# Two hybrid decoder layers on one core: whole-array products with zero rows and columns, one exponent matrix per delta head, and the sample attention's packed products in one run

## The chip, the core and the metric

The kernel runs on one core of a Trainium2 chip. The metric is the device time of one execution in microseconds (us), median of several runs. The core has five engines with a queue each: TensorE (PE; its weight loads are listed apart as PEld), VectorE (DVE), ScalarE (ACT), GpSimd (POOL) and SyncE (SP), which in this kernel issues nearly all DMAs.

## What is computed

Two layers of a decoder, for a prompt of 512 tokens and for 8 samples of 8 tokens (64 tokens); model width 1024, all float32. A layer does this:

```
h = rmsnorm(x);  one input projection, cut into the inputs of three branches and three gates
A: 4 heads HGRN2, gated linear recurrence, per-channel decay
B: 4 heads differential attention (two halves of 64 per head), QK norm, rotary;
   a sample also attends to 1024 past positions in paged caches
C: 4 heads gated DeltaNet: conv, l2 norm of q and k, per-head decay g, and per block of 128 tokens
   D = exp(G_t - G_s);  A = beta D (k k^T), strictly lower;  U = (1 + A)^-1 beta (v - e^G k S)
   o = e^G q S + ((q k^T) D) U
x = x + (sum of sigmoid(gate) * (branch @ w_branch)) @ w_out
x = x + (silu(conv(g)) * u) @ w_down        with g, u = rmsnorm(x) @ w_up
```

Outputs are the new x, the final states of the branches, the new key and value rows and the convolution histories.

## The kernel before, in words

All 576 tokens (512 and 64) stand in the free dimension, 128 channels on the partitions. **Dense products** (`dense_steps`, L265) make one output tile of 128 channels: the float32 weights are loaded by SP (`raw`), split into a high and a low float32r part by ACT (`wh`) and DVE (`wl`), and for each of the K blocks six matmuls of 288 columns run on the whole 128x128 array (two halves of the tokens, three products of high and low parts). Such a matmul is called a dense pass below. One tile of `w_out`, the first of layer 0, is cut in 512 and 64 columns instead (`wide`).

**The branch stage** of a layer mixes the 68 tiles of the input projection with everything that the branches need. `drive` (L319) is a planner that runs while the program is written: it has three lanes of Python generators (left and right: the heads; `smp`: the samples one after another, as soon as the attention heads have ended) and a clock that counts estimated PE time. A head says `yield 4.2` when its next step should come 4.2 us of that clock later, or asks for a dense tile with `yield win(i)`; in between, the planner emits dense passes, one K block at a time, gates and output gates (`fill`) when no head asks. What the program is handed to afterwards is a tile scheduler that may still change the order of instructions on an engine.

The **small products** of the heads are plain float32. Each shows in the trace as two passes (a float32 transpose is one). They use the array in several shapes, which the trace gives as rows*columns: 128*128 (whole), fewer rows where a product sums over 64 tokens (or over 15 bf16 rows), fewer columns where the left operand has 64 of them, and 128*32 or 64*128 or 32*128 where several products are packed side by side (`tile_position`). PSUM for them is `rp()`, four banks in turn.

What the change touches:

- `transpose_to` (L470) and `transpose_back` (L485): four transposes of 128 tokens, and one for the 64 sample tokens.
- `gdn_head` (L752): `parts` (L784) cuts an exponent vector into three bf16 parts, `weights` (L795) transposes them (`pst`), spreads them over the partitions by five products with 15 rows (`sel`, `rt`), multiplies k by k (call 0) or k by q (call 1) and applies exp. Call 0 is followed by the triangular solve of 16x16 blocks: `da` goes to DRAM and back, 30 DVE instructions on `dtr` (L855), `dt` and `ct` to DRAM and back, then `TB`, whose first use on PE is L913. Call 1 comes after the solve in the code, behind `yield 1.0` and `yield 4.5`; `yield 1.0` and `yield 11.0` come before `TB` is used.
- `gdn_head`'s end (L974 to L984): two products of 64x64 for the samples. `hgrn_head` (L990): `level` (L1026) has a sample product with 64 columns at three of its seven levels, and `ATs` (L1119) one of 64x64.
- `diff_head`: `scores` (L1204), two packed products of 64 rows for each of four query blocks, then softmax.
- `diff_sample` (L1256), for each sample: K pages loaded, `sn` (new keys, packed 128*32), `yield 7.0`, `sc` for the first four pages, `yield 7.0`, V pages 0, `sc` for the other four, softmax, V pages 1, transposes, `po` (packed; its last step has 64 rows), `ob`, `yield 1.2`, a packed product with `comb`. The four products `sn`, `sc`, `sc`, `comb` are apart from each other.

Of the kernel before, what the change touches and what calls it, by code (L numbers as in the profile page):

```python
# [10 lines left out]
F32 = mybir.dt.float32  # L11
# [17 lines left out]
HALF = T // 2  # L29
PAST = 1024  # L30
# [115 lines left out]
def kernel(ctx, tc, a, o, depth=DEPTH, dbg=None):  # L146
# [118 lines left out]
    def dense_steps(src, xs, M=128, raws=None, nk=None, prime=False, wide=False):  # L265
# [23 lines left out]
        for g, (k0, n) in enumerate(gr):  # L289
            wh, wl = nxt  # L290
            for i in range(n):
# [4 lines left out]
                for w, xx in ((wh, (xh, xl)), (wl, (xh,))):  # L296
                    for hf in range(2):
                        for x_ in xx:
                            ts = (slice(0, SEQ), slice(SEQ, T))[hf] if wide else slice(hf * HALF, (hf + 1) * HALF)
                            mm(acc[:M, hf, :ts.stop - ts.start], w[:, cs], x_[:, ts],  # L300
                               start=(k == 0 and w is wh and x_ is xh), stop=(k == nk - 1 and w is wl))
# [3 lines left out]
        if wide:  # L305
            return acc.rearrange('p a b -> p (a b)')[:, 0:T].rearrange('p (a b) -> p a b', a=2)
        return acc[:, :, :HALF]

    def dense(src, xs, wide=False):
        return run(dense_steps(src, xs, wide=wide))  # L310
# [119 lines left out]
    def norm_sq(k, xt, sqp, sa):  # L430
        if k == 0:
            S.activation(sa, xt, AF.Square)
        else:
            sq = sqp.tile([128, T], F32, tag='sq', bufs=2, name='sq')
            S.activation(sq, xt, AF.Square)
            tt(sa, sa, sq, ALU.add)
# [4 lines left out]
    def norm_stats(sa, rb, r):  # L441

        ps = rp()
        for j in range(5):
            n = 128 if j < 4 else NS
            mm(ps[:n, j:j + 1], sa[:, 128 * j:128 * j + n], ones[:, 0:1])
# [23 lines left out]
    def transpose_to(dst, src, scale=None):  # L470
# [4 lines left out]
        trp(ps2[:NS, 0:128], src[:, SEQ:], ident)  # L475
        G.memset(dst[NS:, 4, :], 0.0)
        if scale is None:
            S.copy(dst[:, 0:4, :], ps.rearrange('p (j d) -> p j d', j=4))
            S.copy(dst[:NS, 4, :], ps2[:NS, 0:128])
# [3 lines left out]
        S.activation(dst[:NS, 4, :], ps2[:NS, 0:128], AF.Copy, scale=scale[:NS, 4:5])  # L483

    def transpose_back(src):  # L485
# [4 lines left out]
        trp(ps2[:, 0:NS], src[:NS, 4, :], ident[:NS, :NS])  # L490
        return ps, ps2[:, 0:NS]

    def head_norm(ot, p):
# [10 lines left out]
    def finish_gated(ot, key, src, gcol, dst, p, tag):  # L504
# [3 lines left out]
        head_norm(ot, p)  # L508
# [81 lines left out]
    with stage('ln0', 'right') as p0:  # L590
        sa = p0.tile([128, T], F32, tag='sqa', name='sqa')
# [45 lines left out]
    for l in range(depth):  # L637
# [10 lines left out]
        bh = lay.tile([128, 5, 4], F32, tag='bh', name='bh')  # L648
# [4 lines left out]
        GB = lay.tile([128, 5, 4], F32, tag='GB', name='GB')  # L653
        GC = lay.tile([128, 5, 4], F32, tag='GC', name='GC')
# [19 lines left out]
        def decays(p):  # L674
# [9 lines left out]
            S.activation(bh, sp[:, :, 0:4], AF.Exp, scale=-1.0)  # L684
            V.tensor_scalar(out=bh, in0=bh, scalar1=0.5, scalar2=None, op0=ALU.mult)
# [3 lines left out]
            lab = lay.tile([NS, NB, 4], F32, tag='lab', name='lab')  # L689
            tt(lab, bc1(la[:NS, 4, :], NB), bc(c['bm8'][:NS], 4), ALU.mult)  # L690
# [4 lines left out]
            mm(ps[:, 32:64], ones[:NS, :], lab.rearrange('p b e -> p (b e)'))  # L695
            mm(ps[:NS, 64:68], c['trib'][:NS], la[:NS, 4, :])
            mm(ps[:NS, 68:72], c['oneb'][:NS], la[:NS, 4, :])
# [6 lines left out]
            tt(GB, Gt, sp[:, :, 0:4], ALU.subtract)  # L704
            V.tensor_scalar(out=GC, in0=Gt, scalar1=-0.5 * math.log(128.0), scalar2=None, op0=ALU.add)
            V.tensor_scalar(out=nG, in0=Gt, scalar1=-1.0, scalar2=None, op0=ALU.mult)
# [45 lines left out]
        def gdn_head(h, p):  # L752
            ckq = p.tile([128, 2, T], F32, tag='ckq', name='ckq')
            cv = p.tile([128, T], F32, tag='hn', name='cv')
            sel = c['sel'].rearrange('p (j t) -> p j t', j=5)
            mad = c['madd'].rearrange('p (a t) -> p a t', a=2)
# [858 lines left out]
```

## Time and profile before

| | us |
|---|---|
| median of 3 runs (2520.1 to 2521.52) | 2520.16 |
| the profiled execution, its own time | 2517.85 |
| its span from first to last instruction | 2516.1 |
| PE busy / DVE busy / ACT busy / POOL busy | 2492.3 / 1677.5 / 1134.2 / 119.3 |
| branch stage of layer 0 and of layer 1 (from the span's start) | 5.8 to 717 and 1266 to 1966 |

The granted TensorE clock is 0.999 of full speed. In a row of the timeline the first number is the start from the span's beginning, the second how long the row lasts, and xN the number of instructions in it. Matmul ends are modelled and overlap the next ones, so PE's cost of something is read from starts: from a start ahead of it to a start behind it, less what else was started in between.

### The profile page before, as it was taken

The numbers are of one execution on the slowest core, as the hardware profiler recorded it, in microseconds if no ns is written. First come the engines' busy times: TensorE is split into PE (matmuls) and PEld (weight loads), VectorE is DVE, ScalarE is ACT, GpSimd is POOL, SyncE is SP. The second block draws the span as 40 slices with busy tenths as digits, with TensorE's granted clock in tenths as the row PEclk, the third lists the DMA queues.
The fourth block names the chain that finished last, engine by engine and source line by source line (L and its number), as shares of the span: only waits on it lengthen the run. The fifth ranks groups of instructions, "written<-read, shape, count | busy, mean of one in ns | idle before, by whom it ended". The sixth has DMA issues, their size and how long they took to land.

```text
span 2516.1 us, 52047 instructions
## 1 busy us (share of the span) xinstructions
PE 2492.3 (99%) x19714; PEld 2338.6 (93%) x19714; DVE 1677.5 (67%) x4218; ACT 1134.2 (45%) x2435; POOL 119.3 (5%) x378
## 2 busy tenths in 40 slices
PE   8999999999999999999999999999999999999999
PEld 7898888888899999999998988888889999999999
DVE  7777777777765663646676877777686656636463
ACT  5556555556433332323455565646464333323232
POOL 1000000000000010101000000000000000101010
PEclk9999999999999999999999999999999999999999
DMA  6233464545365324242432235554534653242423
GB/s 206 88 109 120 141 202 133 181 156 177 104 213 173 133 85 159 85 146 95 137 130 95 96 121 181 168 176 148 180 129 160 192 176 119 86 159 82 159 85 124
DMA packets 222843, 352.93 MB, mean 140 GB/s; under 512 B 36864, under 2 KB 71680, under 8 KB 222592
## 3 DMA queue, kind: packets, MB, share of 16 engines
q1 hardware_dynamic: 221008, 346.78, 42.3%
q8 instruction: 156, 2.56, 0.4%
q10 hardware_dynamic: 1584, 2.82, 0.4%
q14 instruction: 95, 0.78, 0.1%
HBM read 288.90 MB, written 60.60 MB: 139 GB/s over the span
## 4 chain that ended last, share of the span: by engine, by line
PE 93%; DVE 4%; ACT 2%; issue 1%; DMA 0%; SPq 0%; ACTq 0%; DVEq 0%
PE acc L188 75%; PE r L188 14%; PE r L192 4%; DVE mx L1216 1%; DVE wl L195 0%; ACT P L1219 0%; DVE r L195 0%; DMA x<-in_xT 0%; DVE mx L1289 0%; DMA pg<-in_v 0%; ACT ks L777 0%; DVE ca L743 0%; DVE thb L723 0%; DVE xl L427 0%; DVE ro L195 0%
## 5 line engine op out<-in xcount | busy, mean ns | idle before, releaser
L188 PE MATMUL acc<-xh,wh 128*128 128x288 f32 x3584 | 1026.1, 301 | 2.9 <-DVE thb L710 1.6
L188 PE MATMUL acc<-xl,wh 128*128 128x288 f32 x3584 | 1010.7, 297 | 1.0 <-DVE xl L427 0.9
L188 PE MATMUL acc<-xh,wl 128*128 128x288 f32 x3584 | 773.3, 296 | 5.3 <-DVE wl L195 5.3
L262 ACT CAST wh<-raw 128x512 fp32r<-128x512 f32 x624 | 383.5, 615 | 841.0 <-PE acc L188 791.8
L188 PEld LDWEIGHTS acc<-xh,wh 128*128 128x128 f32 x3584 | 674.5, 188 | 33.8 <-issue 19.4
L188 PEld LDWEIGHTS acc<-xl,wh 128*128 128x128 f32 x3584 | 675.5, 188 | 6.4 <-issue 2.9
L188 PEld LDWEIGHTS acc<-xh,wl 128*128 128x128 f32 x3584 | 576.7, 188 | 11.9 <-DVE wl L195 6.5
L195 DVE TENSOR_TENSOR wl<-raw,wh 128x512 fp32r<-128x512 f32 x624 | 423.2, 679 | 187.7 <-ACT wh L262 183.7
L188 PE MATMUL acc<-hl,wh 128*128 128x288 f32 x704 | 197.5, 296 | 0.0
L188 PE MATMUL acc<-hh,wh 128*128 128x288 f32 x704 | 196.7, 294 | 0.0
L188 PE MATMUL acc<-hh,wl 128*128 128x288 f32 x704 | 150.7, 295 | 0.0
L188 PEld LDWEIGHTS acc<-hh,wh 128*128 128x128 f32 x704 | 132.2, 188 | 0.0
L188 PEld LDWEIGHTS acc<-hl,wh 128*128 128x128 f32 x704 | 132.0, 188 | 0.0
L188 PEld LDWEIGHTS acc<-hh,wl 128*128 128x128 f32 x704 | 113.9, 189 | 0.0
L188 PE MATMUL acc<-oL,wh 128*128 128x288 f32 x384 | 108.0, 295 | 0.0
L188 PE MATMUL acc<-oh,wh 128*128 128x288 f32 x384 | 107.3, 295 | 0.0
L195 DVE TENSOR_TENSOR cbf<-acc,rb 128x288 f32<-128x288 f32 x132 | 39.1, 352 | 90.2 <-PE acc L188 86.3
L1456 DVE SCALAR_TENSOR_TENSOR caf<-cbf,fm,caf 128x592 f32<-128x592 f32 x88 | 73.5, 835 | 15.1 <-ACT caf L1454 13.5
L188 PE MATMUL acc<-oh,wl 128*128 128x288 f32 x384 | 81.6, 293 | 0.0
L1412 DVE SCALAR_TENSOR_TENSOR xn<-acc,xo 128x576 f32<-128x576 f32 x40 | 30.3, 758 | 73.3 <-PE acc L188 73.3
L188 PEld LDWEIGHTS acc<-oL,wh 128*128 128x128 f32 x384 | 73.0, 190 | 0.0
L188 PE MATMUL acc<-mh,wh 128*128 128x288 f32 (+2 forms) x256 | 72.3, 296 | 0.0
(415 smaller groups left out, 3665.5 us busy)
## 6 DMA issues: line engine op xcount, KB each, us to landing
raw<-in_w_in_t SPq DMA_DIRECT2D x272, 256.0 KB
raw<-in_w_up SPq DMA_DIRECT2D x176, 256.0 KB
pg<-in_kT SPq DMA_DIRECT2D x128, 256.0 KB
pg<-in_v SPq DMA_DIRECT2D x128, 256.0 KB
raw<-in_w_dn SPq DMA_DIRECT2D x64, 256.0 KB
xo<-xres SPq DMA_DIRECT2D x56, 288.0 KB
thd<-thb SPq DMA_DIRECT2D x48, 288.0 KB
th<-thd SPq DMA_DIRECT2D x48, 288.0 KB
```

What stands on the lines that cost most here:

```text
L188: PE.matmul(out, lhsT, rhs, start=start, stop=stop, **kw)
L192: PE.transpose(out, in_, idm)
L195: (eng or V).tensor_tensor(out=out, in0=in0, in1=in1, op=op)
L262: S.copy(hi, src)
L1216: V.tensor_reduce(out=mx[:, cc:cc + 1], in_=pss[cc][:, :nk], axis=AX.X, op=ALU.max)
L1412: V.scalar_tensor_tensor(out=v2(xn), in0=acc, scalar=0.5, in1=v2(xo), op0=ALU.mult, op1=ALU.add)
L1456: V.scalar_tensor_tensor(out=A[:, 0:592], in0=P[:, j:j + 592], scalar=w[:, 3 * fi + j:3 * fi + j + 1], in1=A[:, 0:592], op0=ALU.mult, op1= ...
```

## The change

1. `wide` goes; the first tile of `w_out` is made like the others.
2. Operands of the sample products get zero rows or columns up to 128 (`TP = SEQ + 128` columns, memsets on POOL), and the products run on the whole array: the sample's transposes, `level`'s sample products, `Rs`/`TS`, `Us`/`aps`, `Vs`, the norm sums, `gsum`, part of `decays`. `ATs` is packed in 32 columns like the products that it is added to.
3. `gdn_head` makes one exponent matrix. `weights` is called once, `sel` has 128 rows, its five products stand in a run, and k is multiplied by k and q together (256 columns). What differs between the two old matrices is a factor per token, which `head_norm` takes up as `cn`. `yield 4.5` and the second call are gone.
4. `scores` makes query blocks 0 and 1 together.
5. `diff_sample` issues `comb` of the sample before, `sn` and both `sc` in one run, 12.0 after the K pages; V pages 0 are issued behind both `sc`.

```
 transpose_to:
-        trp(ps2[:NS, 0:128], src[:, SEQ:], ident)
-        G.memset(dst[NS:, 4, :], 0.0)
+        trp(ps2[:, 0:128], src[:, SEQ:], ident)
 transpose_back:
-        trp(ps2[:, 0:NS], src[:NS, 4, :], ident[:NS, :NS])
+        trp(ps2[:, 0:128], src[:, 4, :], ident)
 head_norm:
+        for _ in range(0 if cn is None else 2):
+            tt(ms, ms, cn, ALU.mult)
...
+        if cn is not None:
+            tt(r, r, cn, ALU.mult)
 gdn_head:
+            G.memset(ckq[:, :, T:], 0.0)
+            G.memset(cv[:, T:], 0.0)
...
-                trp(pst[:15, 0:128], pc.rearrange('p a j -> p (a j)'), identb)
+                trp(pst[:, 0:128], pc, identb)
...
-                pb, pg = rp(), rp()
+                pb, pg = rp(), (rp(), rp())
+                for j in range(4):
+                    mm(pb[:, 128 * j:128 * j + 128], sel[:, j, :], rt)
                 for j in range(4):
                     cs = slice(128 * j, 128 * j + 128)
-                    mm(pb[:, cs], sel[:15, j, :], rt)
-                    mm(pg[:, cs], ckq[:, 0, cs], ckq[:, i, cs])
+                    mm(pg[j // 2][:, 256 * (j % 2):256 * (j % 2) + 256].rearrange('p (i t) -> p i t', i=2), ckq[:, 0, cs], ckq[:, :, cs])
...
-            pc = parts(1)
+            cn = sm.tile([128, 5], F32, tag='cn', name='cn')
+            tt(cn, ss[:, 0], ss[:, 1], ALU.subtract)
...
-            yield 4.5
-            yield from weights(1, pc)
...
-            mm(pu[:NS, 0:128], TTs, Rs)
+            mm(pu[:, 0:128], TTs, Rs)
...
-            mm(pu[:NS, 0:128], aps[:, 1], Us)
+            mm(pu[:, 0:128], aps[:, NS:], Us)
 hgrn_head:
-                    mm(ps[:NS, :NS], lhs[:, SEQ:], rhs[:, SEQ:])
+                    mm(ps[:, :NS], lhs[:, SEQ:], rhs[:, SEQ:T])
...
-            mm(pu[:NS, 0:128], ATs, vt[:NS, 4], stop=False)
+            for q in range(2):
+                mm(pu[32 * q:32 * q + 32, 0:128], ATs[:, 32 * q:32 * q + 32], vt[:, 4], stop=False, tile_position=(0, 32 * q))
 diff_head:
-            nxt = scores(0)
+            nxt = scores(0, 1)
             for qb in range(4):
-                yield 4.2
-                P, rl = nxt
+                if qb != 1:
+                    yield 5.4 if qb == 0 else 4.2
+                P, rl = nxt.pop(0)
 diff_sample:
             Kp = [pages('K', g) for g in range(2)]
...
+            yield 12.0
             sn = rp()
+            put = combine(b - 1, sn) if b else None
             for h in range(H):
...
-            for g in range(2):
-                yield 7.0
-                if g:
-                    Vp.append(pages('V', 0))
+            scs = []
+            for g in range(2):
                 sc = rp()
                 for h in range(H):
                     mm(sc[32 * h:32 * h + 32].rearrange('p (k t) -> p k t', k=4), Qs[:, b, h, :], Kp[g][:, :, 128 * h:128 * h + 128],
                        cost=0.24, tile_position=(0, 32 * h))
+                scs.append(sc)
+            if b:
+                put()
...
+            Vp = [pages('V', 0)]
...
-                        mm(po[hs], PT[:NS, i, hs], Vs[:, h], start=False, stop=True, tile_position=(0, 32 * h))
+                        mm(po[hs], PT[:, i, hs], Vs[:, h], start=False, stop=True, tile_position=(0, 32 * h))
...
+            mm(pn[q_, 0:128], c['comb'], obs.pop(b), tile_position=(0, 32 * (b % 4)))
+            return lambda: S.copy(on[q_, b // 4], pn[q_, 0:128])
```

## Rows read from the trace of the kernel before

**Rows 1.** The page: busy time, and a group of dense passes with PE's idle before it.

```profile
PE 2492.3 (99%) x19714; PEld 2338.6 (93%) x19714; DVE 1677.5 (67%) x4218; ACT 1134.2 (45%) x2435; POOL 119.3 (5%) x378
...
L188 PE MATMUL acc<-xh,wl 128*128 128x288 f32 x3584 | 773.3, 296 | 5.3 <-DVE wl L195 5.3
```

**Rows 2.** Busy time by stretch, the two branch stages; columns as named: us, engines, clock.

```profile
5.80:717.00 711.20, 699.27 (x5710) 624.02 (x5709) 532.43 (x1610) 393.16 (x948) 32.41 (x98) 1.00 0.46 151
...
1266.00:1966.00 700.00, 693.26 (x5710) 620.02 (x5709) 520.05 (x1573) 384.31 (x932) 24.68 (x88) 1.00 0.45 146
```

**Rows 3.** PE timeline: first and second tile of `w_out`, layer 0, then layer 1.

```profile
793.25 0.39 PE L188 MATMUL acc<-mh,wh 128*128 128x512 f32 x1
...
801.41 0.38 PE L188 MATMUL acc<-mh,wh 128*128 128x288 f32 x1
...
2042.00 0.30 PE L188 MATMUL acc<-mh,wh 128*128 128x288 f32 x1
...
2048.34 0.29 PE L188 MATMUL acc<-mh,wh 128*128 128x288 f32 x1
```

**Rows 4.** PE timeline: a small product on the whole array between dense passes.

```profile
442.30 0.38 PE L188 MATMUL r<-S,ckq 128*128 128x128 f32 x2
...
442.79 0.29 PE L188 MATMUL acc<-xh,wh 128*128 128x288 f32 x1
```

**Rows 5.** PE timeline: a small product on 64*64 between dense passes.

```profile
327.29 0.29 PE L188 MATMUL acc<-xh,wh 128*128 128x288 f32 x1
327.50 0.43 PE L188 MATMUL r<-Us,aps 64*64 64x128 f32 x2
...
328.10 0.29 PE L188 MATMUL acc<-xh,wh 128*128 128x288 f32 x1
```

**Rows 6.** PE timeline: one `sc` of a sample, packed 128*32, between dense passes.

```profile
229.90 0.43 PE L188 MATMUL acc<-xh,wl 128*128 128x288 f32 x2
230.26 1.07 PE L188 MATMUL r<-pg,Qs 128*32 128x512 f32 x8
...
231.49 0.29 PE L188 MATMUL acc<-xl,wh 128*128 128x288 f32 x1
```

**Rows 7.** PE timeline: `weights`, call 0, between two times four transposes.

```profile
253.35 0.60 PE L192 MATMUL r<-cf,P 128*128 128x128 f32 x4
253.88 0.23 PE L188 MATMUL r<-rt,cb_c 15*128 15x128 bf16 x1
...
257.01 0.38 PE L188 MATMUL acc<-xh,wh 128*128 128x288 f32 x1
```

**Rows 8.** PE timeline: `weights` where the four `rt` came in a run.

```profile
386.61 0.39 PE L188 MATMUL r<-rt,cb_c 15*128 15x128 bf16 x4
...
388.43 0.53 PE L188 MATMUL acc<-xh,wl 128*128 128x288 f32 x2
```

**Rows 9.** PE timeline: five transposes, the fifth on 64 rows (64*128).

```profile
68.30 0.80 PE L192 MATMUL r<-cf,ro 128*128 128x128 f32 x5
...
69.27 0.30 PE L188 MATMUL acc<-xl,wh 128*128 128x288 f32 x1
```

**Rows 10.** PE timeline: five transposes, the fifth to 64 columns (128*64).

```profile
48.30 0.71 PE L192 MATMUL r<-cf,xr 128*128 128x128 f32 x5
...
48.98 0.30 PE L188 MATMUL acc<-xl,wh 128*128 128x288 f32 x1
```

**Rows 11.** SP's waits: us in total, times, longest; V and K pages waiting for PE.

```profile
SPq L1264 <- PE r L188: 104.4, 41, 10.3
```

**Rows 12.** DVE timeline: part of the solve, and call 1's `dd` of the same head.

```profile
386.16 1.03 DVE L195 TENSOR_TENSOR dtr<-dtr 36x15 f32<-36x15 f32 x5
387.12 0.34 DVE L809 SCALAR_TENSOR_TENSOR dd<-r,w,cb_c 128x128 f32<-128x128 f32 x1
```

**Rows 13.** DVE and PE timeline: `TB` made, and its first use.

```profile
289.58 0.89 DVE L195 TENSOR_TENSOR TB<-ctt,cf 128x128 f32<-128x128 f32 x4
...
289.94 0.63 PE L188 MATMUL r<-TB,ap 128*128 128x64 f32 x4
```

More of the change, by code (lines that the diff above doesn't have):

```diff
@@ L304, in dense_steps, with dense @@
                     yield
-        if wide:
-            return acc.rearrange('p a b -> p (a b)')[:, 0:T].rearrange('p (a b) -> p a b', a=2)
         return acc[:, :, :HALF]
-    def dense(src, xs, wide=False):
-        return run(dense_steps(src, xs, wide=wide))
+    def dense(src, xs):
+        return run(dense_steps(src, xs))
     def run(g):
@@ L834, in gdn_head @@
             acc = yield win(4 * h + 2)
-            yield from weights(0, pc)
+            yield from weights(pc)
             cm = p.tile([128, 5, 16], F32, tag='cm', name='cm')
@@ L1023, in hgrn_head @@
             AT = p.tile([128, 4, 128], F32, name='AT')
-            ATs = p.tile([NS, NS], F32, name='ATs')
+            ATs = p.tile([128, NS], F32, name='ATs')
+            G.memset(ATs[NS:], 0.0)
             def level(lhs, rhs, m):
@@ L1202, in diff_head, with scores, softmax @@
             G.memset(ot[:, 4, :], 0.0)
-            def scores(qb):
-                nk = 128 * (qb + 1)
-                pss = [rp(), rp()]
+            def scores(*qbs):
+                pss, out, at = [rp(), rp()], [], 0
+                for qb in qbs:
+                    nk = 128 * (qb + 1)
+                    for cc in range(2):
+                        fs = slice(64 * cc, 64 * cc + 64)
+                        mm(pss[cc][:, at:at + nk], qT[fs, 128 * qb:128 * qb + 128], kT[fs, :nk], cost=nk / 600, tile_position=(64 * cc, 0))
+                    at += nk
+                at = 0
+                for qb in qbs:
+                    nk = 128 * (qb + 1)
+                    out.append(softmax([ps[:, at:at + nk] for ps in pss], nk))
+                    at += nk
+                return out
+            def softmax(pss, nk):
                 mx = sm.tile([128, 2], F32, tag='mx', name='mx')
@@ L1209, in scores @@
                 P = p.tile([128, 2, SEQ], F32, tag='P', bufs=2, name='P')
-                for cc in range(2):
-                    fs = slice(64 * cc, 64 * cc + 64)
-                    mm(pss[cc][:, :nk], qT[fs, 128 * qb:128 * qb + 128], kT[fs, :nk], cost=nk / 600, tile_position=(64 * cc, 0))
                 for cc in range(2):
@@ L1416 @@
         with stage(f'ln2{l}', 'right') as p2:
-            sa = p2.tile([128, T], F32, tag='sqa', name='sqa')
+            sa = p2.tile([128, TP], F32, tag='sqa', name='sqa')
             xs = []
             for f in range(KD):
-                acc = dense(a['w_out'][l, f], mixs, wide=(l, f) == (0, 0))
+                acc = dense(a['w_out'][l, f], mixs)
                 x_ = residual(f, acc, xsrc if l == 0 else xres, xres, p2)
@@ L1479 @@
                 p0 = nst.__enter__()
[L1480 removed]
+                sa = p0.tile([128, TP], F32, tag='sqa', name='sqa')
                 xs, xt = [], []
```

221 lines of the change are left out of this document (111 added, 110 removed).

## The prediction

> **What bounds the kernel.** I read the page first: PE is busy 2492.3 of a span of 2516.1, no other engine over 67% [rows 1]. The busy times by stretch then say where anything can move: outside the two branch stages PE runs dense passes only, and inside them it still idles just 11.9 and 6.7 us (711.20 less 699.27, 700.00 less 693.26) [rows 2]. So the time is PE's, and the change is worth what it takes out of PE's queue, less what PE then has to wait for. The question is what a small product really costs there, and its modelled duration doesn't tell: the pair in rows 4 and the pair in rows 5 last 0.38 and 0.43. Starts tell. 48 dense passes of a tile took 6.34, 0.132 each [rows 3]. A float32 product of 128 columns on the whole array (two passes), with two dense passes behind it, took 0.49 from its start, so 0.23 [rows 4]. One of the same length on 64*64 took 0.81 from the dense pass ahead to the second one behind, less two dense passes 0.55 [rows 5]. The difference, 0.32, is a **toll**: what PE pays to leave the whole-array shape and come back. A packed `sc` pays it too: 1.59 less three dense passes is 1.19, of which 0.32 toll and 0.87 work, 0.435 for a pass of 512 columns [rows 6]. The change is mostly a removal of tolls, so I count visits.
>
> **The delta heads.** Call 0 of `weights` goes in and out of the 15-row shape five times: from 253.35 to 257.01 are 3.66, less eight transposes of 0.11 (five took 0.68 less one dense pass, 0.55) 2.8 [rows 7, 10]. Two of the 16 calls had their four `rt` in a run and took 1.8 [rows 8]. Before: 14 times 2.8 and 2 times 1.8, 42.8. After, 8 calls: four bf16 products in a run, 0.3 (in rows 8 they are over within 0.39); eight passes of 256 columns, which no row shows: between the 0.115 of a 128-column pass and the 0.435 of a 512-column one [rows 4, 6], and as the latter grows with the columns I take half of it, 0.215, together 1.7; the sample part 0.3. That is 2.3 a head, 18.4 in all: **24.4 saved**. The transposes of the exponents to 15 rows are visits of their own, 16 tolls of 0.32, and become 8 instructions of some 0.06: **4.6**.
>
> **Sample transposes.** Five transposes with the fifth on 64 rows took 0.97 less a dense pass, 0.84; with a fifth on the full rows 0.55 [rows 9, 10]. 32 of them (two per attention head, one per delta and HGRN2 head, two layers) at 0.29: **9.3**.
>
> **The sample attention.** For each sample `comb`, `sn` and two `sc` are four visits and become one; the first sample of a layer has no `comb` ahead of it. That is 2 and 7 times 3 tolls a layer, 46 in all at 0.32: **14.7**. The last step of `po` goes from 64 to 128 rows, half a toll (one change of shape in place of two) 16 times: **2.6**.
>
> **Other products.** `Rs` and `Us`, 16 times 0.32: **5.1**. `ATs` in the shape of its neighbours, 8 halves: **1.3**. `level`'s sample product, 24 times: the toll goes, but two passes with 128 columns of weights replace two with 64; I take 0.2 of 0.32: **4.8**. Two score blocks together, one visit fewer in 8 heads: **2.6**. Norm sums, `gsum` and `decays`, 8 visits, of which I count half since they stand beside other changes of shape: **1.3**. The cut `w_out` tile took 8.16 against 6.34 [rows 3]: **1.8**.
>
> **Sum on PE: 72.5.**
>
> **What lies beside.** POOL gets some 33 more small memsets a layer. Its 98 instructions took 32.41 in a stage of 711, 0.33 each, so 11 us a layer on an engine that is idle 95% [rows 2]; without that cover it would be 11 a layer. DVE and ACT lose call 1 (four `dd` of 0.34 on DVE among it [rows 12]) and get four half products for two, and a few five-column instructions for `cn`: I count nothing, and DVE's 532 us, spread over some 36 fewer, go from 75% to 79% of the stage. `weights` holds four PSUM banks where it held three; a lane that wants one waits for an exp.
>
> SP: V pages 0 can't be issued before the first `sc` has read their buffer. They were issued 7.0 of the planner's clock after it, and are now issued right behind both products. SP runs ahead, so it will stand there longer; the weights' `raw` loads stand behind it, as do stores and state loads. It already stands at the pages 41 times, 104.4 in all and up to 10.3 at a time [rows 11], yet dense passes waited just 5.3 in the whole kernel for split weights [rows 1]: the prefetched tiles cover such a stop. I count nothing; without that cover it would be up to 7 for each of 16 samples. K pages come 1.2 earlier behind `po`, and their product 12.0 later, in place of 0 and 7.0: more cover, not less.
>
> **PE's idle time.** The tolls were also time in which DVE and ACT caught up with PE. PE's 18.6 us of idle time in the two stages can stay (0) or double; I take 7 more, over a third, since the engines that fill it lose work too.
>
> So 72.5 less 7, **65.5** from the profiled execution's 2517.85, which gives 2452.4. The median of the runs stands 2.3 above that execution: **2455**.
>
> **Rivals.**
>
> *PE catches up with the heads* (10%). DVE at 79% of a stage serves three lanes in order, and each of its delays now meets a PE that is 36 us a layer earlier. If the idle time triples (37 more, not 7), the time is 2485. For it: several waits of PE in these stages end at DVE. Against: there were 431 us of dense passes a layer (68 tiles of 6.34) to lay in between, before as after.
>
> *The runs don't stay runs* (10%): the scheduler lays other work between the packed products, as it laid call 1's `dd` into the solve that stands well ahead of it in the code [rows 12]. Then the 46 tolls and the 8 of the score blocks are paid as before: 17.3 more, 2472.
>
> *The solve is late* (4%), the one that ends slower. In the code, `TB` is used after 14 us of clock behind call 0, where 22 lay before (the second call, `yield 4.5` and 0.7 are gone). The data needs longer: `TB` was made at 289.58, 33 us after a call 0 that began at 253.88 and took 2.8 [rows 7, 13]. If PE stood there in code order, it would wait 33 less 15.4 (14 of the clock, at 0.132 for its 0.12 a pass), some 18 us, in each of 8 heads: 144 more, 2599. It decides from 8.1 us a head (65.5 over 8). Against it: with 22 of clock, 24 us, PE would have stood there 9 us a head before the change, 72 us in all, and it idled 18.6 in both stages; `TB`'s use at 289.94 followed its making with dense passes ahead of it [rows 13]. The order is made by readiness.
>
> *Narrow transposes pay too* (4%). If each of the 80 transposes to 64 columns also cost a toll, the change would take 25.6 more: 2429. Rows 10 speak against it: five transposes, the last of them to 64 columns, took 0.55, five times 0.11. In the Trainium skill the page "TensorEngine Tiling (Array Packing)", section Tiling Modes, lists 128x64 among the modes and says that a change of mode drains the engine; by that this rival would be the forecast. The trace agrees with it for products [rows 5, 6], not for these transposes.
>
> **Chances and range.** The forecast has the remaining 72%. About 0.2% of the time, 5 us, is what a measurement can tell from no change. All cases but the late solve are far below that line; of its 4% I give 3 to slower and 1 to a wait that just eats the gain. So faster 96%, same 1%, slower 3%. Low end: no new idle time (7), the 256-column passes at 0.115 (64 of them, 6.4), `level` and the norm sums at a full toll (4.2): 2437. High end: those passes at 0.435 (14), idle time doubled (12 more): 2481, rounded up to 2482. That holds the split runs too; left out are the tripled idle time, the late solve, the narrow transposes and the forecast's tails, about 2 in 10.
>
> **What would show it.** PE's busy time some 72 lower, and all of it between 5.8 and 717 and in the second branch stage, each 30 to 36 shorter; the dense stages unchanged but for `w_out`'s first tile at 6.3. No more 15-row and 64*64 products; a delta head's `weights` at 2.3; five transposes at 0.55 everywhere; one run of `comb`, `sn`, `sc`, `sc` of about 2.5 a sample. Wrong in size: 256-column passes not at 0.215, or packed runs with dense passes in them. Wrong in kind: PE's idle time well over 26 in the two stages, ended by `TB`, by `wl` (late `raw`), or by PSUM banks behind `weights`.

## The result, and the profile after

| | before | after |
|---|---|---|
| median of the runs on the same chip, us | 2520.84 | 2451.43 (2448.3 to 2452.74, 4 runs) |
| the profiled execution, us | 2517.85 | 2451.43 |
| span, us | 2516.1 | 2449.6 |

The ratio is 0.9721, with a 95% interval of 0.9705 to 0.9738: 2.8% faster. The forecast was 2455, within 2437 to 2482. The time is right, but it came from other places than forecast, and that is what the rest is about.

The busy times of the page after and a group of dense passes with PE's idle time before it, to be held against [rows 1]:

```profile
PE 2420.2 (99%) x19602; PEld 2317.4 (95%) x19602; DVE 1664.6 (68%) x4156; ACT 1119.8 (46%) x2401; POOL 131.9 (5%) x446
...
L189 PE MATMUL acc<-xh,wl 128*128 128x288 f32 x3584 | 767.0, 294 | 5.0 <-DVE wl L196 4.7
```

PE is busy 72.1 less, as the forecast wanted (72.5 of work). By stretch it reads otherwise. Busy time by stretch of the kernel after (us, then PE, PEld, DVE, ACT, POOL, granted clock, DMA share, GB/s): branch stage, branch products, `w_out` and FFN of layer 0, then of layer 1.

```profile
6.80:688.20 681.40, 667.38 (x5654) 617.30 (x5653) 525.35 (x1577) 384.53 (x930) 38.44 (x130) 0.99 0.49 157
688.20:764.40 76.20, 76.20 (x578) 76.20 (x577) 47.32 (x70) 20.33 (x33) 0.15 (x1) 1.00 0.59 181
764.40:815.00 50.60, 50.60 (x387) 50.60 (x386) 27.56 (x39) 20.16 (x32) 0.41 (x2) 1.00 0.56 181
815.00:1229.10 414.10, 414.10 (x3184) 413.62 (x3183) 241.98 (x411) 141.70 (x220) 30.56 (x91) 1.00 0.37 118
1229.10:1904.60 675.50, 665.20 (x5654) 617.24 (x5653) 513.87 (x1542) 377.58 (x914) 30.30 (x117) 0.99 0.47 151
1904.60:1980.80 76.20, 76.20 (x578) 76.20 (x577) 47.27 (x70) 20.33 (x33) 0.15 (x1) 1.00 0.59 180
1980.80:2031.40 50.60, 50.60 (x387) 50.60 (x386) 27.57 (x39) 20.16 (x32) 0.33 (x2) 1.00 0.55 182
2031.40:2445.70 414.30, 414.27 (x3184) 413.57 (x3182) 230.65 (x395) 130.93 (x204) 29.30 (x84) 1.00 0.36 115
```

The same view of the kernel before, for the two stages after the branch stage that changed (those of [rows 2] were 711.3 and 700.1 from end to end):

```profile
793.20:846.30 53.10, 53.10 (x387) 52.05 (x386) 27.57 (x39) 20.13 (x32) 0.33 (x2) 1.00 0.52 174
846.30:1265.70 419.40, 419.40 (x3184) 418.89 (x3183) 242.15 (x411) 141.54 (x220) 29.72 (x90) 1.00 0.35 116
...
2042.00:2092.60 50.60, 50.60 (x387) 50.60 (x386) 27.62 (x39) 20.13 (x32) 0.33 (x2) 1.00 0.54 183
2092.60:2512.20 419.60, 419.59 (x3184) 418.84 (x3182) 230.95 (x395) 131.05 (x204) 29.32 (x84) 1.00 0.35 114
```

The branch stages gave 29.9 and 24.6, `w_out` of layer 0 gave 2.5, and each FFN stage gave 5.3, with the same 3184 instructions on PE, which is busy from end to end in both. The start took 1.0 more. In all 66.6; the spans differ by 66.5. So **the branch stages gave 54.5 where 63.7 was forecast** (70.7 of work there, the 1.8 of `w_out` left out, less 7 of idle time), **and 10.6 came from two stages that the change doesn't touch.**

The pieces of the branch stages look as forecast. The one `weights` of a delta head, `pb` in a run, eight passes of 256 columns, then the sample part (timeline of PE):

```profile
249.92 0.40 PE L189 MATMUL r<-rt,cb_c 128*128 128x128 bf16 x4
250.15 1.95 PE L189 MATMUL r<-ckq 128*128 128x256 f32 x8
251.93 0.22 PE L189 MATMUL r<-rt,cb_c 128*128 128x128 bf16 x1
251.99 0.44 PE L189 MATMUL r<-ckq 128*128 128x128 f32 x2
...
252.40 0.30 PE L189 MATMUL acc<-xl,wh 128*128 128x288 f32 x1
```

From 249.92 to 252.40, less one dense pass, are 2.35; forecast 2.3. The eight passes start 1.78 / 8 = 0.22 apart, the half of a 512-column pass that was assumed. Five transposes on full rows and a sample's packed run, in the same view (the scheduler mixes `ob`, `kTs` and `pg` among each other, but they share one shape and no dense pass comes between them):

```profile
68.64 0.71 PE L193 MATMUL r<-cf,ro 128*128 128x128 f32 x5
...
69.33 0.29 PE L189 MATMUL acc<-xl,wh 128*128 128x288 f32 x1
...
358.38 0.30 PE L189 MATMUL r<-ob,cf 128*32 128x128 f32 x1
...
358.73 1.88 PE L189 MATMUL r<-pg,Qs 128*32 128x512 f32 x13
360.54 0.40 PE L189 MATMUL acc<-xh,wh 128*128 128x288 f32 x1
360.78 0.30 PE L189 MATMUL acc<-xl,wh 128*128 128x288 f32 x1
```

0.69 less a dense pass is 0.56 for the transposes that took 0.84 [rows 9]; the run takes 2.40 less 0.13, 2.3, where the four visits, an `sc` of 1.2 [rows 6] twice among them, took 3.1 (49.2 in the table below, over 16 samples).

Summed over every start in the branch stages of both traces (from an instruction's start to the next one's, less 0.132 for a dense pass next to a small product, and without what a semaphore made late), the groups of small products stand so, in us:

| group | before | after | saved | forecast |
|---|---|---|---|---|
| `rt`, `ckq` of `weights` | 43.3 | 18.8 | 24.5 | 24.4 |
| transposes of the exponents | 5.4 | 1.0 | 4.5 | 4.6 |
| transposes back (`ro`, `ot`) | 30.9 | 21.7 | 9.2 | 9.3 |
| `comb`, `sn`, `sc` | 49.2 | 32.8 | 16.4 | 14.7 |
| `po` | 36.9 | 35.7 | 1.2 | 2.6 |
| `Rs`, `Us` | 8.4 | 4.7 | 3.7 | 5.1 |
| `ATs` and the products that it is added to | 10.2 | 10.9 | -0.7 | 1.3 |
| `level` (all on `XX`) | 59.0 | 55.7 | 3.4 | 4.8 |
| scores (`qT`) | 29.0 | 28.7 | 0.4 | 2.6 |

Each is within some 2 us of its term. The small products as a whole (the stages' time less dense passes at their mean pitch, which is the time from one start to the next, less waits) fell by 63.6.

**What ate the difference** is waiting. PE's visible idle time in the two stages went from 18.7 to 24.3 (us less busy in the rows), 5.7 more where I had taken 7. But much waiting doesn't show as idle time, as here (timeline of PE after, a `level` of HGRN2):

```profile
493.53 0.42 PE L189 MATMUL acc<-xh,wl 128*128 128x288 f32 x2
493.78 0.29 PE L189 MATMUL acc<-xh,wh 128*128 128x288 f32 x1
494.10 1.33 PE L189 MATMUL r<-XX 128*128 128x128 f32 x10
```

`XX` starts 0.32 behind the last dense pass, where 0.13 is usual, yet no idle time is named: the modelled end of that pass, 494.07, covers it. Counting, at instructions that waited for a semaphore, each start that is over 40 ns later than the usual one for its pair of shapes, waits in the branch stages rose from 41.0 to 51.8: **10.8 more, only half of it visible.** (The hidden part hangs on what is taken as usual: with the median of a pair's starts the rise is 8 to 9.) And a visible wait can cost twice, by the clock (timeline of PE, then the stretch behind it by 2 us; the granted clock is the third column from the right):

```profile
1828.94 0.43 PE L189 MATMUL r<-TB,ap 128*128 128x64 f32 x2 [1.74 <-DVE TB L196]
```

```profile
1828.00:1830.00 2.00, 1.06 (x8) 1.06 (x9) 1.41 (x7) 0.00 (x0) 0.00 (x0) 0.93 0.82 254
1830.00:1832.00 2.00, 2.00 (x12) 2.00 (x11) 0.44 (x4) 0.60 (x1) 0.00 (x0) 0.50 1.00 338
1832.00:1834.00 2.00, 2.00 (x11) 2.00 (x10) 0.54 (x2) 0.00 (x0) 0.00 (x0) 0.50 0.22 82
1834.00:1836.00 2.00, 2.00 (x10) 2.00 (x10) 1.09 (x3) 0.29 (x1) 0.00 (x0) 0.50 0.00 0
1836.00:1838.00 2.00, 2.00 (x18) 1.98 (x16) 0.95 (x2) 1.36 (x4) 0.00 (x0) 0.87 0.00 0
```

PE waits 1.74 for `TB`, some 10 us after a wait of 0.98 that an instruction of a solve on DVE ended, and behind it the granted clock is at the lower of its two levels, 1.2 GHz: what the five rows lack to 1.00, times 2, is 3.4 us. The kernel before has nothing of the kind in layer 1; in layer 0 both kernels have two drops, near 30 and near 400, that cost 1.7 each. Length alone doesn't decide it. The longest waits of the stages after, one in each layer, have the upper level behind them (timeline of PE, then the stretch around it):

```profile
468.84 0.40 PE L189 MATMUL acc<-xh,wh 128*128 128x288 f32 x1 [2.04 <-ACT wh L263]
```

```profile
460.00:480.00 20.00, 17.82 (x134) 16.98 (x132) 16.63 (x46) 14.75 (x32) 2.98 (x7) 1.00 0.50 165
```

Nor does the drop come with every execution: of the four after, three had a mean granted clock of 0.997 and the fourth, 3.1 us shorter, 0.999. Of 33 further executions of the kernel before, the 12 at 0.999 took 2517.9 in the mean and the 5 at 0.996 took 2523.1. The profiled execution before is one at 0.999, that after one at 0.997. So the 3 us by which the profiled difference (66.4) stays behind that of the medians (69.4) can be of this kind, and whether the change brings the drop in layer 1 is not shown: the trace of experiment 1, with PE's instructions of before, has one of 1.7 there too.

So 63.6 of work, with 1.6 from a slightly shorter mean pitch of the dense passes, less 10.8 of waits, is the 54.5; in the 63.6 the clock's 3.4 are already lost, so the work alone was some 67 of the 70.7.

### The profile page after: what moved, and what is told of

Its sections match the earlier page's. It is cut to its first block, busy times and chain, and to the rows that moved or that the text cites. A ratio compares the mean times of both kernels' runs of the same rounds, so it can differ in the third digit from the quotient of the medians.

```text
span 2449.6 us, 51852 instructions
## 1 busy us (share of the span) xinstructions
PE 2420.2 (99%) x19602; PEld 2317.4 (95%) x19602; DVE 1664.6 (68%) x4156; ACT 1119.8 (46%) x2401; POOL 131.9 (5%) x446
## 3 DMA queue, kind: packets, MB, share of 16 engines
q10 hardware_dynamic: 1584, 2.82, 0.4%
## 4 chain that ended last, share of the span: by engine, by line
PE 89%; DVE 6%; ACT 3%; issue 1%; DMA 1%; SPq 0%; ACTq 0%; DVEq 0%
PE acc L189 72%; PE r L189 13%; PE r L193 3%; DVE dtr L196 1%; DVE wl L196 1%; DMA ctt<-dt 0%; DVE XX L196 0%; DVE s L527 0%; DVE ca L737 0%; ACT wh L263 0%; DMA x<-in_xT 0%; ACT P L1235 0%; ACT ks L773 0%; DMA og<-ogd 0%; DVE ot L196 0%
## 5 line engine op out<-in xcount | busy, mean ns | idle before, releaser
L189 PEld LDWEIGHTS acc<-oh,wh 128*128 128x128 f32 x384 | 72.1, 188 | 0.0
```

What stands on the lines that cost most here:

```text
L189: PE.matmul(out, lhsT, rhs, start=start, stop=stop, **kw)
```

## The experiments

**1. Where the FFN's 10.6 came from.** In starts (timeline of PE, FFN of layer 0; pairs of rows that are six passes apart, two pairs of the kernel before, then one of after):

```profile
900.24 0.29 PE L188 MATMUL acc<-xh,wh 128*128 128x288 f32 x1
...
901.02 0.29 PE L188 MATMUL acc<-xh,wh 128*128 128x288 f32 x1
...
1200.40 0.29 PE L188 MATMUL acc<-xh,wh 128*128 128x288 f32 x1
...
1201.19 0.29 PE L188 MATMUL acc<-xh,wh 128*128 128x288 f32 x1
```

```profile
1200.26 0.29 PE L189 MATMUL acc<-hh,wh 128*128 128x288 f32 x1
...
1201.04 0.29 PE L189 MATMUL acc<-hh,wh 128*128 128x288 f32 x1
```

Six passes took 780 ns at 900 and 790 at 1200, on the same `xh`; after the change, 780 throughout. Such a steady time is called a rhythm below. In the kernel before, the 780 end at the first pass that reads `hh` (948.6); from there it is 790 with `xh` and 790 or 800 with `hh`. One thing about `hh` had changed: other tiles grew and shrank, and the program places it 384 bytes a partition higher, at byte 123648 in place of 123264 (256 in place of 384 in 512 bytes; the tiles of `hh` lie 2304 bytes apart, so each second one lies 256 off that). So only the place was changed:

```
         ph = hst.__enter__()
+        pad = ph.tile([128, (96, 32)[l]], F32, name='pad')
+        G.memset(pad[:, 0:1], 0.0)
```

> The kernel before, with one unused tile at the head of the pool of the FFN's hidden tiles: 384 bytes a partition in layer 0 (hh then lies at the address that it has after the change) and 128 bytes in layer 1. No instruction of PE is added or taken away. Theory P (the dense pass keeps one of several rhythms, 780, 790 or 800 ns for six passes, and reading hh at its old address throws it out of the fastest): in layer 0 all six-pass blocks of the FFN stay at 780 as they do after the change, and the stage of 419.4 us gets 5.3 shorter; layer 1 gets 5.3 shorter too if the old address alone is bad, and stays at 419.4 if the new one alone is good. In all 2510 or 2515.5 us. Rival H (the rhythm comes from what PE did before the FFN, the branch stage or w_out, and not from where hh lies): both FFN stages stay at 419.4, in all 2520.8.

Measured: 2508.93 against 2518.81, ratio 0.9959 (0.9945 to 0.9973). The FFN stages of layer 0 and layer 1:

```profile
847.60:1261.90 414.30, 414.30 (x3184) 413.79 (x3183) 241.92 (x411) 141.39 (x221) 29.53 (x90) 1.00 0.36 118
...
2090.10:2504.60 414.50, 414.48 (x3184) 413.74 (x3182) 230.69 (x395) 130.96 (x204) 29.35 (x84) 1.00 0.35 115
```

Theory P holds and H falls: 5.1 off in each layer by moving a tile, 384 bytes or 128. The old place is bad: in all ten traces here that have x and `hh` at 0 and 256 and the old order of the passes, those that read `hh` take 780. **Ten of the change's 69 us are luck of placement**, to be had in the kernel before without any of its edits.

**2. Which places are bad.** The operands of the dense stages are moved in the kernel after, each layer by another amount:

```
         pm = mxs.__enter__()
+        pad = pm.tile([128, (32, 64)[l]], F32, name='pad')
...
+        pad = pmix.tile([128, (32, 96)[l]], F32, name='pad')
         mst.__exit__(None, None, None)
...
         ph = hst.__enter__()
+        pad = ph.tile([128, (32, 416)[l]], F32, name='pad')
```

> The kernel after with unused tiles that move the operands of the dense stages, and nothing else: the FFN's hidden tiles by 128 bytes a partition in layer 0 (the old place plus 512) and by 1664 in layer 1 (the old place plus 2048), the operands of w_out by 128 and 256, those of the branch products by 128 and 384. Theory P512 (the old place was bad for where it lies in 512 bytes): the FFN stage of each layer is 5 us longer again (six passes at 790 or 800), 2461. P2048: layer 1 alone, 2456. Theory Q (one bad place among many, or not the address by itself): both FFN stages stay at 414.1, 2451. For the others nothing is known ahead; if their passes can come down to 780 ns for six, the branch products (76.2 us a layer, 793 for six) gain 1.3 us a layer and w_out (50.6, 790) 0.6.

Measured: 2458.45, ratio 0.9763 (0.9744 to 0.9782). FFN of layer 0 and 1:

```profile
811.90:1231.20 419.30, 419.30 (x3185) 418.82 (x3184) 242.13 (x411) 141.84 (x220) 30.75 (x90) 1.00 0.35 117
2030.90:2450.60 419.70, 419.65 (x3185) 418.94 (x3183) 230.87 (x396) 131.09 (x204) 29.68 (x84) 1.00 0.35 114
```

P512: both stages are as slow as before the change, with `hh` at its old place plus 512 and plus 2048. What counts is the place within 512 bytes (or a part of it). The branch products went from 76.2 to 76.8, six passes from 793 to 800.

**3. The normed x, moved.**

```
-    xp = pool('xp', bufs=8)
+    xq = pool('xq', bufs=1)
+    xp = pool('xp', bufs=8)
+    xr_ = pool('xr', bufs=1)
...
+    for q, n in ((xq, 32), (xr_, 96)):
+        pad = q.tile([128, n], F32, name='pad')
+        G.memset(pad[:, 0:1], 0.0)
```

> The kernel after with the normed x (xh, xl, operands of the dense passes in the branch stage and of w_up) 128 bytes a partition higher, and all that lies behind it on that side by 512. In the branch stages six dense passes take 780, 790 or 807 ns, 790 in the mean, and keep what they have between two visits of other products. Theory A (where x lies against the weights sets which of them is taken): the mean leaves 131.7 a pass by over 1, so each branch stage changes by 3 us or more, and the FFN leaves 414.1. Rival M (the moment at which PE comes back sets it): the mean stays within 0.4 of 131.7, the stages change by less than 3.

Measured: 2462.54, ratio 0.976 (0.9744 to 0.9777). The FFN is 419.4 in both layers: `xh` at 384 in 512 throws the passes out of 780 as `hh` did there. In the branch stages the mean pitch is 131.99 in both, 0.3 from 131.70, and the stages (683.3 and 674.6) stay within 2, as M wanted. The mean hides a change. Of the stretches of six passes with no other product and no visible wait in them, 30% (layer 0) and 31% (layer 1) took 780 after the change, 11% and 14% took 807, and 6% and 5% took 800; with x moved, 1% and 1% take 780, 1% and 1% take 807, and 19% and 20% take 800. With x at its old place and the old order of the passes, every other trace has 20 to 37% at 780, so M's moment has its part too. But A is right in kind in the branch stages as well as in the FFN: where x lies sets which rhythms occur. In the branch stages gains and losses nearly cancel in the mean, and the mean was M's mark.

**4. The split run.** The sample's packed products apart again, with the yields of before:

```
-            yield 12.0
             sn = rp()
-            put = combine(b - 1, sn) if b else None
...
-            scs = []
+            Vp = []
             for g in range(2):
+                yield 7.0
+                if g:
+                    Vp.append(pages('V', 0))
                 sc = rp()
...
-            if b == NB - 1:
-                yield 1.2
-                combine(b, rp())()
+            yield 1.2
+            combine(b, rp())()
```

> The kernel after, with the sample attention's four packed products apart again, with the yields of before (sn at once, sc 7.0 later, V pages 0 and sc 7.0 after that, comb 1.2 behind po). Nothing of the computation changes. Theory T (a visit to another array shape costs 0.32 us, so 46 tolls were saved): 14.7 us slower, 7.4 in each branch stage, 2466. Rival W (what the run saved was handed back as waiting for DVE and ACT, so that splitting it only fills idle time): at most 5 us slower, with PE's idle time in the branch stages some 8 lower. If it is over 20 slower, the run also saved waits.

Measured: 2464.42, ratio 0.9777 (0.9754 to 0.98). The branch stages:

```profile
6.30:697.40 691.10, 676.04 (x5652) 617.43 (x5653) 524.02 (x1578) 386.72 (x931) 39.38 (x130) 0.99 0.47 154
1238.30:1919.30 681.00, 672.76 (x5654) 615.82 (x5653) 511.60 (x1542) 378.56 (x914) 30.88 (x117) 0.99 0.46 150
```

9.7 and 5.5 more, 15.2 in all: theory T, 14.7. Idle time is 15.1 and 8.2 in place of 14.0 and 10.3, so the tolls were no filling of idle time (W falls). Work without waits and dense passes rose by 16.1, 0.35 for each of the 46; 1.7 of it is the clock, at the lower level for 6.8 us around 410 where the kernel after has 3.4, and without that it is 0.31.

**5. Old shapes of the transposes**, one kind in each layer (`transpose_back`, `transpose_to`):

```
-        trp(ps2[:, 0:128], src[:, 4, :], ident)
+        if l == 0:
+            trp(ps2[:, 0:NS], src[:NS, 4, :], ident[:NS, :NS])
+        else:
+            trp(ps2[:, 0:128], src[:, 4, :], ident)
...
-        trp(ps2[:, 0:128], src[:, SEQ:], ident)
+        n = 128 if l == 0 else NS
+        trp(ps2[:n, 0:128], src[:, SEQ:SEQ + n], ident)
```

> The kernel after with old transposes of the 64 sample tokens: in layer 0 the transposes back to channels read 64 rows as before (16 of them: 8 in the attention heads, 8 at the end of the delta and HGRN2 heads); in layer 1 the transposes to tokens write 64 columns as before (20 of them). Theory T: five transposes back take 0.84 again in place of 0.55, so the branch stage of layer 0 is 16 times 0.29, 4.6 us longer; layer 1 is unchanged, 0 us, since a narrow transpose pays no toll. Rival N (narrow transposes pay a toll as the products do, the page rule on array modes): layer 1 is 20 times 0.32, 6.4 us longer as well. In all 2456 against 2462.5.

Measured: 2449.89, ratio 0.9722 (0.9706 to 0.9739), as fast as after.

```profile
6.70:690.70 684.00, 670.66 (x5655) 617.54 (x5653) 524.91 (x1577) 385.41 (x931) 38.78 (x130) 1.00 0.48 156
1231.60:1902.20 670.60, 663.15 (x5655) 615.32 (x5654) 513.29 (x1542) 377.38 (x915) 34.05 (x136) 1.00 0.47 152
```

Layer 0 is 2.6 longer; its work is 4.3 longer, as T says (4.6), and 1.5 of waits went. By the count of starts above, the transposes back take 15.3 in place of 10.9. Layer 1, where N wanted 6.4 more, is 4.9 shorter. Its work without waits fell by 0.9; 3.9 of waits are gone, and the clock drop of 3.4 shrank to one of 1.7 elsewhere, behind the same wait for `wh` that had none after the change. By the count of starts the transposes to tokens take 18.4 in this layer in both kernels. N falls. The layer also shows what a stage time is worth here: an edit that should do nothing moves it by 5, through the waits that happen to arise.

**6. The 15-row products**, interleaved in layer 0, in a run in layer 1:

```
-                for j in range(4):
-                    mm(pb[:, 128 * j:128 * j + 128], sel[:, j, :], rt)
+                for j in range(4 if l else 0):
+                    mm(pb[:, 128 * j:128 * j + 128], sel[:15, j, :], rt[:15])
                 for j in range(4):
                     cs = slice(128 * j, 128 * j + 128)
+                    if l == 0:
+                        mm(pb[:, cs], sel[:15, j, :], rt[:15])
...
-                mm(pb[:, 0:128], sel[:, 4, :], rt)
+                mm(pb[:, 0:128], sel[:15, 4, :], rt[:15])
```

> The kernel after with the delta heads' five spreading products on 15 rows again: in layer 0 each of the first four stands ahead of its product of k with k and q (five visits to the 15-row shape a head), in layer 1 the first four stand in a run (two visits a head). The transposes of the exponents stay on the whole array, and the result is the same. Theory T (the visit costs, not the product): layer 0 five times 0.32 in 4 heads, 6.4 us longer; layer 1 two times 0.32 in 4 heads, 2.6 us longer; 9 in all, 2460. Rival R (the narrow rows make the product itself slow, so both layers lose the same for their 20 products): the two layers get longer by the same time. Rival W (idle time takes it up): under 3 in all.

Measured: 2457.12, ratio 0.9753 (0.9734 to 0.9771). Layer 0 got 10.6 longer (692.0), layer 1 3.6 shorter (671.9). A `weights` by itself, where nothing stands beside it, takes 3.72 to 3.79 in layer 0 and 2.82 in layer 1, for 2.35: 1.4 for five visits, 0.47 for two. R falls, since the same products cost three times as much when apart; T holds in kind, with 0.23 to 0.28 a visit in place of 0.32. The rest of layer 0's 10.6 are waits and a drop of the clock (620 to 640, 0.83 in the mean), and layer 1 lost its own drop, which had only shrunk in experiment 5.

**7. Another order of the six passes.**

```
-                for w, xx in ((wh, (xh, xl)), (wl, (xh,))):
-                    for hf in range(2):
-                        for x_ in xx:
+                o = [(w, x_, hf) for w, x_ in ((wh, xh), (wh, xl), (wl, xh)) for hf in range(2)]
+                if order[0]:
+                    o = [(w, x_, hf) for hf in range(2) for w, x_ in ((wh, xh), (wh, xl), (wl, xh))]
```

> The kernel after with another order of the six dense passes of a block: in layer 0 the two halves of the tokens take turns (wh xh, wh xh, wh xl, wh xl, wl xh, wl xh, each for the first and the second half); in layer 1 the first half's three passes come ahead of the second half's three. The sums are the same. Theory C (part of the 130 ns of a pass of 288 columns comes from two passes running on into the same accumulator): layer 0, where none follows on its own, gets faster, at 126 ns by 4 ns for 7392 passes, some 30 us; layer 1, where four of six follow on, gets slower. Rival D (the pass is bound by the weight load and the read of its operand alone): both layers within 10 us of before, by the rhythm that each falls into.

Measured: 2477.74, ratio 0.983 (0.9814 to 0.9847), 26 slower than after. Six passes take 800 nearly everywhere in the dense stages of both layers (branch stages 132.65 and 133.07 a pass, FFN 424.6). C falls: passes that follow on into the same accumulator are not what costs, and the 126 ns that it put for layer 0 stood on no row. D holds in kind, but layer 0 got some 14 slower, beyond its 10 (layer 1 some 10). Each order has rhythms of its own, and the kernel's is the best of the three.

**8. More time ahead of `TB` and of the last transposes.**

```
         head_norm(ot, p, cn)
-        yield 5.0
+        yield 6.0
...
-            yield 11.0
+            yield 15.5
             for m in (16, 32, 64):
```

> The kernel after with more time ahead of two steps of the heads: 15.5 in place of 11.0 of the planner's clock before TB is used (the 4.5 that the change took away), and 6.0 in place of 5.0 ahead of the last transposes of a delta or HGRN2 head. No instruction changes. Theory L (the new idle time is PE coming too early to TB and ot, 3.9 and 2.2 us of idle time in the two stages): these waits go, idle time falls by 4 to 6 and the time by as much, 2446. Rival W (DVE and ACT are behind in these stages as a whole; a wait that is taken away at TB turns up at wh, wl or another head's step): idle time stays within 3 of the 24 us and the time within 3 of 2451.

Measured: 2442.09, ratio 0.9683 (0.9667 to 0.97), 0.4% faster than after and the fastest version seen.

```profile
6.20:686.40 680.20, 666.30 (x5653) 617.57 (x5653) 521.93 (x1573) 383.40 (x926) 38.06 (x128) 0.99 0.47 155
1235.00:1901.70 666.70, 659.67 (x5652) 613.21 (x5652) 510.42 (x1530) 378.49 (x914) 29.53 (x117) 1.00 0.47 152
```

More than L wanted, and not its way: layer 1 gave 8.8, layer 0 1.2. PE still waits for `TB`, 1.1 and 1.0 us in two heads, and for `ot`, 0.45 in two; idle time fell by 3.4 only, all of it in layer 1, where the clock now stays up. A wait turned up elsewhere too, as W has it: 3.1 us in each layer, at 364.3 and 1569.8, for `XX` on DVE (L704), longer than any in the branch stages after the change. Behind the first the clock is at 1.2 GHz for 6.8 us, behind the second it is not.

**9. The branch operands on a multiple of 256 bytes, and the two halves of experiment 8.** `aligned` is the kernel after with `oh` and `oL` 224 bytes lower, at 0 and 256 in 512; `tb_lead` adds the 15.5, `lead_aligned` both yields, and `norm_lead` is the kernel after with the 6.0 alone.

```
+        pad = pmix.tile([128, 56], F32, name='pad')
+        G.memset(pad[:, 0:1], 0.0)
         mst.__exit__(None, None, None)
```

> The kernel after with one unused tile of 224 bytes a partition, which brings the operands of the branch products (oh, oL) to multiples of 256 bytes; before, and 128 and 384 lower, they lay at other offsets and took 793, 800 and 800 ns for six passes. Theory A256 (an operand that starts on a multiple of 256 bytes leaves the fastest rhythm alone; hh and x did so at 256 and 0 in 512, and were thrown out at 384): the branch products come to 780, 75.0 in place of 76.2 us a layer, and w_out, whose own operands are on such multiples and which only kept what it found, to 780 as well, 49.9 in place of 50.6; 3.8 in all, 2447.6. Rival H (w_out and the branch products are at 790 for what went before them or for their four blocks a tile): 76.2 and 50.6 stay, 2451.

> The aligned kernel with only the first half of the edit that brought 9 us: 15.5 in place of 11.0 of the planner's clock before TB is used; the last transposes of a head stay at 5.0. Theory TB (that wait was worth it, for the solve is late): as fast as with both, some 9 below the aligned kernel. Theory F (it was the transposes behind the head norm, which got two instructions more): no faster than the aligned kernel, within 2 us. Theory O (neither wait: any shift of the heads lays the lanes in another order, and times of single stages move by up to 5 us with it): anywhere between, the gain in one layer and not the other.

> The aligned kernel with both longer yields, 15.5 and 6.0: the version put together from the experiments. If the two gains add (9.3 from the yields, 3.8 from the place of the branch operands): 2438, 13 below the kernel after and 82 below the one before. If the place does nothing: 2442. If the gain of the yields was the order of one schedule alone, it is the same here, as the unused tile moves no instruction of the branch stage.

> The kernel after with only the second half of the edit that brought 9 us: 6.0 in place of 5.0 of the planner's clock between a delta or HGRN2 head's norm and its last transposes; 11.0 before TB as after the change. Theory F (the norm got three small DVE instructions with cn and the transposes behind it stood waiting for it): PE's waits for ot, 0.45 to 0.61 us in four heads, go, and the time comes to some 2442. Theory O (a shift lays the lanes in another order, and it was the two shifts together): 2445 to 2452, with the waits for ot gone or not.

Measured: 2449.13 (0.9711 to 0.9738), 2448.96 (0.9712 to 0.9739), 2445.08 (0.9695 to 0.9722) and 2449.28 (0.9708 to 0.9734). In `aligned` the branch products come to 75.8 and 76.4 and `w_out` to 50.6 and 50.5: six passes at 790 throughout, neither the 793 of before nor the 780 of A256. `tb_lead` shows why (branch products and `w_out` of layer 0, then of layer 1):

```profile
690.80:765.70 74.90, 74.90 (x579) 74.90 (x578) 47.25 (x70) 20.38 (x33) 0.15 (x1) 1.00 0.58 183
765.70:815.60 49.90, 49.90 (x386) 49.90 (x385) 27.56 (x39) 20.09 (x31) 0.88 (x2) 1.00 0.55 185
1905.20:1982.70 77.50, 77.50 (x579) 77.50 (x578) 47.24 (x70) 20.34 (x32) 0.15 (x1) 1.00 0.56 178
1982.70:2034.30 51.60, 51.60 (x386) 51.60 (x385) 27.57 (x39) 20.11 (x31) 0.74 (x2) 1.00 0.53 178
```

The same passes on the same places: 780 ns for six in layer 0 (49.9 / 64), 806 in layer 1 (51.6 / 64), each of them unbroken across both stages. On a multiple of 256 bytes the branch products and `w_out` *keep* the rhythm with which they come in from the branch stage; they don't fall into the fastest. A256 was half right, and H half.

Of the two yields, neither shows a gain alone (0.2 and 2.2 us, within the intervals; TB and F fall). Both together gave 9.3 over the kernel after, clear of the intervals, and 4.1 over `aligned`, which is not. That is theory O, as far as it goes: another order of the lanes. The version put together from the experiments, `lead_aligned`, is no faster than experiment 8. Which wait or which neighbourhood of products makes the difference stays open.

## Why the prediction was right, and where not

**Right.** The toll, read from starts: 0.32 forecast, 0.31 to 0.35 when the run is split again, 0.23 to 0.28 for the 15-row visits. The delta heads, 24.4 and 4.6 against 24.5 and 4.5 in the starts of both traces, with `weights` at 2.35 (2.3) and 256-column passes at 0.22. The sample run, 14.7 against 16.4, and 15.2 by undoing it. The transposes back, 9.3 against 9.2, with five at 0.56. The choice between ends at 0.115 and 0.435 for the pass of 256 columns was the largest open price, and growth with the columns was the right rule. Narrow transposes pay nothing, shown now by undoing them. The Trainium skill's rule that a change of mode drains the engine ("TensorEngine Tiling (Array Packing)", section Tiling Modes) fits the products here, at 0.23 to 0.35 a visit, and not these transposes, at 18.4 us with and without.

**Wrong: "outside the two branch stages PE runs dense passes only", so "the dense stages unchanged but for `w_out`'s first tile".** They run only dense passes, but a dense pass has no one price. The prediction took 0.132 from one tile [rows 3]. Each FFN stage came out 5.3 shorter, by the place of `hh`, shown by moving it (experiments 1 and 2). `w_out` of layer 0 gave 2.5 for a forecast 1.8: the tiles behind the cut one ran at 800 for six, those after at 790.

**Mis-sized: "I take 7 more" of idle time.** Visible idle time was 5.7 more, near enough. But the term stood for all that PE would have to wait, and that was 10.8, half of it beneath the modelled ends, plus 3.4 by the clock: 14 in place of 7, with the reserve that the clock's part belongs to the profiled execution. The first rival (PE catches up with the heads) was at work, at a third of its price, and so was the third: waits that `TB` or its solve ended make 4.9 us in both layers together (1.05, 1.12, 0.98 and 1.74), some 1 us each and not 18 a head.

**Small misses.** `po` 1.2 for 2.6, `Rs` and `Us` 3.7 for 5.1, `ATs` nothing for 1.3, `level` 3.4 for 4.8; the two score blocks together, 0.4 for 2.6; the sample run 1.7 more than forecast. "The median of the runs stands 2.3 above that execution" did not hold after the change: both are 2451.43. The branch stages were to be 30 to 36 shorter each; they were 29.9 and 24.6, layer 1 outside. The two errors, 9 in the branch stages and 11 in the FFN, cancel, so the time fell within 4 us of the forecast: that is luck. A sum that comes out right is no proof of its terms.

**Covers that held.** PE's idle time ahead of the passes with `wl` didn't grow (5.3 [rows 1], then 5.0), so the V pages' later issue cost nothing there; POOL's stage went from 32.4 to 38.4 beside other work. One new wait of 2.0 us a layer, for `wh` at 468.8 and 1673.7, stands behind ACT: it has a head's logarithm and the sample's exp of 1088 columns in its queue ahead of the split, each with a table load of 1.28.

## What to carry to other kernels

Price a small product from the starts around it, visit by visit, and count visits to other array shapes: that gave the large terms within a few per cent. Ahead of a change that moves tiles, read the pitch of the dense passes in each stage on its own; where it differs between stages with the same instructions, try the place of the operand before anything else (here 10 us for one unused tile). And when PE gets faster, count the waits that don't show as idle time, and look at the granted clock behind the longer ones, in more than one execution, not only at the gaps.

## What was not expected of the hardware

A dense pass of 288 columns has several steady rhythms, 780, 790, 800 and about 807 ns for six, and in the dense stages it keeps the one it has over hundreds of passes, until something disturbs it. In the branch stages it is often another one behind a visit (in 114 of 197 cases after the change), and which ones occur hangs on the place of x (experiment 3). In the FFN tiles at 384 and 128 in 512 bytes throw it out of 780, tiles at 0 and 256 let it be. For the branch operands 480 gave 793 and 96 and 352 gave 800. The Trainium skill's page "SBUF — State Buffer", section SBUF: two separate sides, has PE on ports of its own where it waits for no one. No run here shows what it is that collides, if anything does, only that the place alone is worth 1.3% of the FFN stages (5.3 of 419.4).

A wait of 1.74 us, with another of 0.98 some 10 us ahead, was followed by over 6 us at 1.2 GHz, which cost 3.4 us: twice the wait itself. Waits of 2.04 in the same trace and of 3.15 in experiment 8 were followed by none. What tells them apart is not shown.
